# Modulation steps moved ahead of the neighbourhood projections, 14 more PE transposes, and an earlier first normalization in a two-layer diffusion step

## The chip, the cores and the metric

The kernel runs on one core of one Trainium2 chip. The metric is the device time of one execution in microseconds (us), the median of the runs shown. The kernel computes in single precision: every float32 operand of a matmul is split into a high and a low part in fp32r, and each product is made of two or three fp32r matmuls.

## The reference, cut to what matters

Two layers work on 384 tokens (128 context tokens and 256 latent tokens, width 1024). Each layer is a half-step SwiGLU FFN, a mixer with three branches, and a second half-step FFN. Every one of these six sublayers first normalizes and modulates its input with a shift and a scale, and multiplies its result by a gate; these come from a conditioning vector by a matrix of 1024 x 9216 in each layer:

```
m = silu(cvec) @ w_ada[l] + b_ada[l]          # split in 9: shift, scale, gate of three sublayers
h = ln_plain(x) * (1 + scale) + shift
x = layernorm(ALPHA * x + 0.5 * gate * swiglu(h), g, b)           # FFN
u = h @ w_in                                                       # mixer
q   = (rmsnorm(u_q) * g) @ w_uq;      k_nope, v = (rmsnorm(u_kv) * g) @ w_ukv      # latent attention
q_n, k_n, v_n = u_na                                               # neighbourhood attention
x = layernorm(ALPHA * x + gate * ((g_f*y_f + g_m*y_m + g_n*y_n) @ w_out), g, b)
```

The product with `w_ada` is wanted for two vectors only (context and latent).

## The kernel before, in words

The 384 tokens are three tiles of 128. The six sublayers run one after the other on TensorE (PE); the tail of one and the head of the next are interwoven in `transition`. All of PSUM is one ring of 8 banks (`psum`), which every matmul group, transpose or not, takes a bank of, until VectorE (DVE) and ScalarE (ACT) have read it.

**Weights.** Every weight comes as a unit: a load on the SP queue (`_load`, L180), a cast to the high part on ACT (`_high`, L188, `whi`), a subtraction for the low part on DVE (`_low`, L193, `wlo`). A first, dry pass records in which order instructions are issued, and a planner places each load and each split some us of PE time ahead of its first use, as far as 26 buffers of 4 KB per partition ("u4") and 22 of 3 KB ("t3") have room. The SP queue keeps this written order, and a load whose buffer is not free holds up all behind it. The other queues are put in order by the framework's scheduler, which takes work roughly in the order in which it was issued and runs ready work of later issue in gaps; in `begin` PE, ACT and DVE keep the written order too.

**Modulation steps.** Shift, scale and gate of all sublayers but the first are computed on DVE, one eighth of a block of 1024 columns at a time. One `ada_step` loads 128 rows of `w_ada` (512 KB on SP, planned 14 us of PE time ahead) and updates two accumulators `acc`, one for each conditioning vector: a multiply (TENSOR_SCALAR) in the first step of a shift or scale block, else a multiply-add (SCALAR_TENSOR_TENSOR). After the eighth step `ada_finish` transposes and sums both accumulators on DVE, and some calls later `ada_place` makes one small matmul and four small additions. `ada_spend(n)` first does such outstanding finishes and then up to `n` steps from the budget of the sublayer: 36 in the first FFN, 12 in the mixer of layer 0, 8 in that of layer 1. When a shift or scale block ends ahead of a gate block, `gate_start` clears two accumulators on GpSimd (POOL) and issues two small loads from its queue.

**The mixer's order.** `mixer_body` turns the latents (`turn_q`, `turn_kv`), does the Fourier branch (`four_tokens`, `four_channels`), makes the queries (`query`, 3 tiles), the keys (`kn`, four pairs of heads), the values (`v`, four tiles), then the Fourier branch's projection (`yb`, 8 chunks of 12 matmuls, each copied by DVE into `mg`), then latent attention with the gates' matmuls as filling, the neighbourhood values (`value`, `nv`), and the neighbourhood projections of queries and keys (`nq`, `nk`), then neighbourhood attention. In each pair of key heads DVE subtracts the low parts `k<-kn` out of PSUM and copies the rotary part `k<-krt`. The kernel before calls `ada_spend(1)` once in each `value`, once ahead of the neighbourhood stage, and once ahead of each of the eight `nq` and `nk` projections: 3 + 1 + 8 = 12 steps in layer 0, and in layer 1 3 + 1 + 4 = 8.

**The start.** `run` has PE transpose the identity 24 times ("warm"), loads x and the conditioning vectors, and `begin` normalizes the three tiles: statistics of both halves of a tile (`bn_stats`), an aggregation, the power -0.5 on POOL (`rstd`), and for tiles 0 and 1 the normalization on ACT (`xn`), issued after the next tile's statistics. Then PE turns tile 0 (`xT`), multiplies the first 128 columns of shift and scale (`ada`), turns tile 1 and 2, and the first FFN's matmuls (`hd`) begin as each eighth of the modulated input is ready. `sel` and `quad` are two small constants made from the identity for the matmul `adat`.

Of the kernel before, what the change touches and what calls it, by code (L numbers as in the profile page):

```python
# [8 lines left out]
F32 = mybir.dt.float32  # L9
F32R = mybir.dt.float32r  # L10
AF = mybir.ActivationFunctionType
ALU = mybir.AluOpType
AX = mybir.AxisListType
# [3 lines left out]
P = 128  # L17
# [71 lines left out]
class Kernel:  # L89
# [279 lines left out]
    def ada_setup(self):  # L369
        self.ada_blocks = [("g", (0, 0)), ("m", (0, 1), 0), ("m", (0, 1), 1), ("g", (0, 1)), ("m", (0, 2), 0), ("m", (0, 2), 1),  # L370
                           ("g", (0, 2)), ("m", (1, 0), 0), ("m", (1, 0), 1), ("g", (1, 0)), ("m", (1, 1), 0), ("m", (1, 1), 1),
                           ("g", (1, 1)), ("m", (1, 2), 0), ("m", (1, 2), 1), ("g", (1, 2))]
        self.ada_pos, self.ada_fin, self.ada_due = 0, [], []
        self.mod = {}
        self.gate_d = {}
        sel = self.fixed([P, 32], F32, "sel")
        self.nc.vector.tensor_reduce(out=sel, in_=self.ident.rearrange("p (q r) -> p r q", q=4), op=ALU.add, axis=AX.X)
        self.quad = self.fixed([P, 4, 32], F32, "quad")
        self.nc.gpsimd.tensor_copy(out=self.quad, in_=sel.unsqueeze(1).broadcast_to([P, 4, 32]))
        self.bad = [self.fixed([P, 72], F32, "bad") for _ in range(DEPTH)]  # L380

    def ada_bias(self, l):
# [240 lines left out]
    def transition(self, prev, nxt, mod):  # L623
# [65 lines left out]
            p()  # L689
        self.inhead = False  # L690

    def begin(self, nxt):
        nc = self.nc
        hf = [self.slot([P, 2, TOK], F32, "hf") for _ in range(4)]
        ns, mvs, rs = [], [], []

        def normal(t):
            n = self.slot([P, D], F32, "xn")
            if t == NT - 1:
                nc.vector.tensor_scalar(out=n, in0=self.x[t], scalar1=mvs[t][:, 0:1], scalar2=rs[t], op0=ALU.subtract, op1=ALU.mult)  # L700
            else:
                mr = self.small(1)
                nc.vector.scalar_tensor_tensor(out=mr, in0=mvs[t][:, 0:1], scalar=-1.0, in1=rs[t], op0=ALU.mult, op1=ALU.mult)
                nc.scalar.activation(out=n, in_=self.x[t], func=AF.Identity, scale=rs[t], bias=mr)
            ns.append(n)

        for t in range(NT):
            mvs.append(self.stats(self.x[t]))
            rs.append(self.rstd(mvs[t][:, 1:2], 1.0, 1e-6))
            if t:  # L710
                normal(t - 1)

        def turn(t, then=None, qs=range(2)):
            for q in qs:
                pt = self.psum("xT")
                for b in range(4):
                    dc = q * 4 + b
                    nc.tensor.transpose(pt[:, b * P:(b + 1) * P], ns[t][:, dc * P:(dc + 1) * P], self.ident)
                if then and q == 0:
                    then()  # L720
                for b in range(2):
                    o, i = hf[2 * q + b][:, :, t * P:(t + 1) * P], pt[:, b * 256:b * 256 + 256].rearrange("p (a b) -> p a b", a=2)
                    if b:
                        nc.scalar.copy(out=o, in_=i)
                    else:
                        nc.vector.tensor_copy(out=o, in_=i)

        piece = {0: 1, 1: 1, 2: 1, 3: 1, 4: 2, 6: 2}
        m = self.mod_tile((0, 0))

        hg = {}

        def shift(dc, *cds):
            h = hf[dc // 2][:, dc % 2]
            if dc not in hg:
                hg[dc] = self.slot([P, TOK], F32, "hg")
            g = hg[dc]
            for cd in cds:
                c = (slice(0, P), slice(P, TOK))[cd]
                sc, sh = m[:, 1, dc, cd:cd + 1], m[:, 0, dc, cd:cd + 1]  # L740
                nc.scalar.activation(out=self.hm[0][:, dc, c], in_=h[:, c], func=AF.Identity, scale=sc, bias=sh)
                nc.vector.tensor_scalar(out=g[:, c], in0=h[:, c], scalar1=sc, scalar2=sh, op0=ALU.mult, op1=ALU.add)
            for cd in cds:
                c = (slice(0, P), slice(P, TOK))[cd]
                nc.vector.tensor_tensor(out=self.hm[1][:, dc, c], in0=g[:, c], in1=self.hm[0][:, dc, c].bitcast(F32), op=ALU.subtract)

        turn(0)
        self.ada_bias(0)
        normal(NT - 1)
        self.held = []  # L750
        ahead = self.ada_first(0, 1)
        nxt.cold_unit(0)
        turn(1, self.high)
        self.ada_first_finish(0, 1, ahead)
        shift(0, 0)
        turn(2, qs=[0])
        shift(0, 1)
        self.low()
        turn(2, qs=[1])
        every = [(t, g) for t in range(NT) for g in range(HG)]  # L760
        for dc in range(KD):
            d1 = dc + 1
            if d1 < KD:
                nxt.cold_unit(d1)
            if dc:
                parts, i, j = [(p, t, g) for t, g in every for p in range(3)], 6, 9
            else:
                parts, i, j = [(p, t, g) for ps, ts in (((0, 1), (0,)), ((0, 1), (1, 2)), ((2,), range(NT))) for p in ps for t in ts for g in range(HG)], 12, 15
            if not dc:
                self.high()  # L770
                self.low()
            nxt.cold_head(dc, parts[:i])
            self.high()
            self.low()
            if d1 in piece:
                ahead = self.ada_first(d1, piece[d1])
            nxt.cold_head(dc, parts[i:j])
            if d1 in piece:
                self.ada_first_finish(d1, piece[d1], ahead)
            if d1 < KD:  # L780
                shift(d1, 0, 1)
            nxt.cold_head(dc, parts[j:])
            while self.held:
                self.high()
                self.low()
        self.held = None
        nxt.cold_finish()
        self.ada_bias(1)
        self.gate_start()
# [179 lines left out]
    def mixer_body(self, ph):  # L969
        nc, I, K, O, l = self.nc, self.I, self.K, self.O, ph.l  # L970
# [60 lines left out]
            ckT.append(kt)  # L1031

        def query(t):
            c = slice(t * P, (t + 1) * P)
            qk = self.slot([P, NH, HQ], F32, "qtok")
            for hh in range(2):
                b = self.psum("q")
                for kc in range(3):
                    w = self.W(("wuq", l, kc), "mla_w_uq", l, kc * P, 1, 0, 768)
                    self.mm3(b[:, 0:384], (qnT[kc][:, 0, c], qnT[kc][:, 1, c]),  # L1040
                             tuple(x[:, 0, hh * 384:hh * 384 + 384] for x in w), kc == 0, kc == 2)
                bv = b[:, 0:384].rearrange("p (h j) -> p h j", h=4)
                qs = qk[:, 4 * hh:4 * hh + 4]
                if t == 0:
                    nc.scalar.copy(out=qs, in_=bv)
                else:
                    nc.scalar.copy(out=qs[:, :, 0:64], in_=bv[:, :, 0:64])
                    self.rope(qs[:, :, 64:96], bv[:, :, 64:96], t - 1, 4)
            qtok.append(qk)
# [11 lines left out]
        k96 = [self.slot([HQ, 2, 512], F32R, "k96") for _ in range(NH)]  # L1061
        w = self.ukv(l, 0)
        for pr in range(4):
            b = self.psum("kn")
            for kc in range(2):
                lhs = tuple(x[:, kc, 2 * pr:2 * pr + 2].rearrange("p a b -> p (a b)") for x in w)
                self.mm3(b, lhs, (ckT[kc][:, 0], ckT[kc][:, 1]), kc == 0, kc == 1)
            for e in range(2):
                kk = k96[2 * pr + e]
                self.split(kk[0:64, 0], kk[0:64, 1], b[64 * e:64 * e + 64, :])  # L1070
                nc.vector.tensor_copy(out=kk[64:96], in_=krt[64:96].bitcast(F32))
        w = self.ukv(l, 1)
        vm = []
        for t in range(4):
            b = self.psum("v")
            for kc in range(2):
                self.mm3(b, (ckT[kc][:, 0, t * P:(t + 1) * P], ckT[kc][:, 1, t * P:(t + 1) * P]),
                         tuple(x[:, kc].rearrange("p a b -> p (a b)") for x in w), kc == 0, kc == 1)
            vm.append(self.split_v(b))
# [74 lines left out]
        for p2 in range(4):  # L1154
            for nme in ("nq", "nk"):
# [6 lines left out]
                if nme == "nq":  # L1162
                    q = self.slot([P, 2, TOK], F32R, "qN")
# [101 lines left out]
    def run(self):  # L1265
        nc, I, K, O = self.nc, self.I, self.K, self.O
# [6 lines left out]
        self.mhalf = self.fixed([P, 1], F32, "mhalf")  # L1273
        nc.vector.memset(self.mhalf, -0.5)

        wp = self.psum("warm")
        for i in range(24):
            nc.tensor.transpose(wp[:, i % 4 * P:i % 4 * P + P], self.ident, self.ident)
        self.mask = self.fixed([P, 64], F32, "mask")
        self.rp = self.fixed([P, 2, 2, 32], F32, "rp")  # L1280
        self.ada_setup()
# [292 lines left out]
```

## Time and profile before

| | us |
|---|---|
| median of 3 runs (1868.36 to 1870.40) | 1869.28 |
| the profiled execution, whole | 1866.74 |
| its span from first to last instruction | 1865.0 |
| PE busy in the span | 1842.9 |
| DVE busy | 1409.0 |
| ACT busy | 785.3 |
| POOL busy | 94.7 |

The mean granted TensorE clock is 0.997 of full. A timeline row gives start and duration in us, engine, line, operation, what is written and read, the count of merged instructions, and in brackets the idle time of the engine ahead of it with what ended it. Most operations are recorded under L77, the helper that issues them, so they are told apart by their tiles.

### The profile page before, as it was taken

To read this page: it belongs to the slowest core of one execution; us is meant where nothing else is said; L and a number is where in the kernel's file an instruction comes from. 1 tells how busy PE (TensorE), PEld (TensorE's weight loads), DVE (VectorE), ACT (ScalarE), POOL (GpSimd) and SP (SyncE) were. 2 spreads that over 40 slices of the span, in tenths; PEclk is the share of its full clock that TensorE was granted. 3 is DMA by queue.
4 is the path that set the end of the run, shared out by engine and by line. 5 is a ranking of instruction groups with operands and counts; after the bars stand their busy time and mean duration, and the time that the engine had idled before them with its cause. 6 is when DMAs were issued, how large, how long until landed. Compare 5 with 4: busy or idle time off the path is not lost. (4 is left out here: it accounts for less than half of the span.)

```text
span 1865.0 us, 27258 instructions
## 1 busy us (share of the span) xinstructions
PE 1842.9 (99%) x10568; PEld 1728.1 (93%) x10568; DVE 1409.0 (76%) x2206; ACT 785.3 (42%) x1305; POOL 94.7 (5%) x115
## 2 busy tenths in 40 slices
PE   8999999999999999999999999999999999999998
PEld 6899998999899999999999999989999998999997
DVE  6788888689997677888876888978798776533345
ACT  4433335556355453332453333355554553533330
POOL 0000002000100010000000000120001000000000
PEclk9999999999999999999999999999999999999999
DMA  9766656234835446666545666542356353444522
GB/s 325 264 224 212 206 209 207 88 102 126 234 109 188 125 148 221 196 226 219 188 159 186 221 220 219 193 157 89 113 177 183 104 190 130 133 135 125 145 92 79
DMA packets 225602, 320.22 MB, mean 172 GB/s; under 512 B 32784, under 2 KB 181888, under 8 KB 225344
## 3 DMA queue, kind: packets, MB, share of 16 engines
q1 hardware_dynamic: 223328, 313.88, 52.5%
q0 software_dynamic: 2112, 4.59, 0.6%
q8 instruction: 83, 1.36, 0.3%
q14 instruction: 47, 0.39, 0.1%
q10 hardware_dynamic: 32, 0.01, 0.0%
HBM read 312.32 MB, written 8.02 MB: 172 GB/s over the span
## 5 line engine op out<-in xcount | busy, mean ns | idle before, releaser
L193 DVE TENSOR_TENSOR wlo<-raw,whi 128x1024 fp32r<-128x1024 f32 (+4 forms) x420 | 488.7, 1181 | 148.7 <-ACT whi L188 68.0
L188 ACT CAST whi<-raw 128x1024 fp32r<-128x1024 f32 (+4 forms) x420 | 420.3, 1020 | 325.9 <-DVE wlo L193 83.7
L77 PE MATMUL w<-hmh,whi 128*128 128x384 f32 x1152 | 388.3, 337 | 0.8 <-ACT sl L77 0.8
L77 PE MATMUL w<-hmh,wlo 128*128 128x384 f32 x1152 | 387.1, 336 | 0.0
L77 PE MATMUL w<-hml,whi 128*128 128x384 f32 x1152 | 387.1, 336 | 0.0
L77 PE MATMUL y<-whi,sT 128*128 128x512 f32 x1050 | 335.1, 391 | 1.7 <-DVE sT L77 1.5
L77 DVE SCALAR_TENSOR_TENSOR acc<-raw,cs,acc 128x1024 f32<-128x1024 f32 x236 | 296.9, 1290 | 28.8 <-DMA raw<-in_w_ada_dram 28.5
L77 PEld LDWEIGHTS y<-whi,sT 128*128 128x128 f32 x1050 | 196.8, 188 | 41.1 <-DVE sT L77 2.1
L77 PEld LDWEIGHTS w<-hmh,whi 128*128 128x128 f32 x1152 | 216.6, 188 | 3.2 <-ACT sl L77 1.1
L77 PEld LDWEIGHTS w<-hml,whi 128*128 128x128 f32 x1152 | 216.6, 188 | 1.9
L77 PEld LDWEIGHTS w<-hmh,wlo 128*128 128x128 f32 x1152 | 216.6, 188 | 0.0
L77 PE MATMUL y<-wlo,sT 128*128 128x512 f32 x525 | 204.2, 389 | 0.0
L77 PE MATMUL g<-hmh,whi 128*128 128x384 f32 x384 | 132.5, 345 | 1.4 <-DVE qN L77 1.4
L77 PE MATMUL g<-hmh,wlo 128*128 128x384 f32 x384 | 129.8, 338 | 1.6 <-DVE wlo L193 1.6
L77 PE MATMUL g<-hml,whi 128*128 128x384 f32 x384 | 129.9, 338 | 0.0
L77 PEld LDWEIGHTS y<-wlo,sT 128*128 128x128 f32 x525 | 98.6, 188 | 18.1
L77 ACT CAST sT<-sl 128x384 fp32r<-128x384 f32 x72 | 37.1, 515 | 183.8 <-DVE sl L77 183.8
L77 PE MATMUL hd<-whi,hmh 128*128 128x256 f32 (+1 forms) x336 | 100.1, 300 | 1.6 <-ACT hmh L77 1.6
L77 PE MATMUL hd<-wlo,hmh 128*128 128x256 f32 (+1 forms) x336 | 99.0, 297 | 0.0
L77 PE MATMUL hd<-whi,hml 128*128 128x256 f32 (+1 forms) x336 | 98.9, 296 | 0.0
L77 ACT ACTIVATE sl<-w 128x384 f32<-128x384 f32 x72 | 35.4, 492 | 110.0 <-PE w L77 109.7
L77 POOL TENSOR_TENSOR st<-st,mhalf 128x1 f32<-128x1 f32 x48 | 43.9, 916 | 689.3 <-DVE st L77 689.2
(271 smaller groups left out, 2952.3 us busy)
## 6 DMA issues: line engine op xcount, KB each, us to landing
raw<-in_ffn_w_dram SPq DMA_DIRECT2D x244, 512.0 KB, 5.0
raw<-in_w_ada_dram SPq DMA_DIRECT2D x128, 512.0 KB, 4.9
raw<-in_w_gate_dram SPq DMA_DIRECT2D x48, 512.0 KB, 4.1
raw<-in_w_in_dram SPq DMA_DIRECT2D x32, 512.0 KB, 6.1
raw<-in_w_ada_dram SPq DMA_DIRECT2D x32, 256.0 KB, 5.9
raw<-in_w_out_dram SPq DMA_DIRECT2D x16, 512.0 KB, 6.8
raw<-gd SPq DMA_DIRECT2D x12, 512.0 KB, 5.1
raw<-in_ffn_w_dram SPq DMA_DIRECT2D x22, 256.0 KB, 5.8
```

The lines of the kernel that those rows point to most:

```text
L77: r = f(*a, **kw)
L188: self.real.scalar.copy(out=hi, in_=r)
L193: self.real.vector.tensor_tensor(out=lo, in0=r, in1=hi.bitcast(F32), op=ALU.subtract)
```

## The change

Three edits. The nine calls of `ada_spend` that come new in `mixer_body` use up the budgets of 12 and 8 earlier: in layer 0 three steps stand ahead of the queries, four ahead of the key pairs, two ahead of values 1 and 3, and the last three in `value` as before; in layer 1 three, four and one, and none is left for `value`. The calls further down stay, with nothing to spend. In `begin` PE transposes the identity 14 more times before anything else of `begin`, tile t-1 is normalized between the two halves of tile t's statistics rather than after them, and `sel` and `quad` are computed after the statistics.

```diff
 ada_setup:
-        sel = self.fixed([P, 32], F32, "sel")
-        self.nc.vector.tensor_reduce(out=sel, in_=self.ident.rearrange("p (q r) -> p r q", q=4), op=ALU.add, axis=AX.X)
+        self.sel = self.fixed([P, 32], F32, "sel")
         self.quad = self.fixed([P, 4, 32], F32, "quad")
-        self.nc.gpsimd.tensor_copy(out=self.quad, in_=sel.unsqueeze(1).broadcast_to([P, 4, 32]))
+    def warm(self, n):
+        wp = self.psum("warm")
+        for i in range(n):
+            self.nc.tensor.transpose(wp[:, i % 4 * P:i % 4 * P + P], self.ident, self.ident)
+
     def begin(self, nxt):
         nc = self.nc
+        self.warm(14)
...
         for t in range(NT):
-            mvs.append(self.stats(self.x[t]))
+            st = self.small(12)
+            for h in range(2):
+                nc.vector.bn_stats(out=st[:, h * 6:h * 6 + 6], in_=self.x[t][:, h * 512:h * 512 + 512])
+                if t and h == 0:
+                    normal(t - 1)
+            mvs.append(self.moments(st, 2))
             rs.append(self.rstd(mvs[t][:, 1:2], 1.0, 1e-6))
-            if t:
-                normal(t - 1)
+        nc.vector.tensor_reduce(out=self.sel, in_=self.ident.rearrange("p (q r) -> p r q", q=4), op=ALU.add, axis=AX.X)
+        nc.gpsimd.tensor_copy(out=self.quad, in_=self.sel.unsqueeze(1).broadcast_to([P, 4, 32]))
...
         def query(t):
+            self.ada_spend(1)
...
         for pr in range(4):
+            self.ada_spend(1)
             b = self.psum("kn")
...
         for t in range(4):
+            self.ada_spend(t % 2)
             b = self.psum("v")
...
 run:
-        wp = self.psum("warm")
-        for i in range(24):
-            nc.tensor.transpose(wp[:, i % 4 * P:i % 4 * P + P], self.ident, self.ident)
+        self.warm(24)
```

## Rows read from the trace of the kernel before

**Rows 1.** The page: busy us of each engine in the span.
```profile
PE 1842.9 (99%) x10568; PEld 1728.1 (93%) x10568; DVE 1409.0 (76%) x2206; ACT 785.3 (42%) x1305; POOL 94.7 (5%) x115
```

**Rows 2.** Stretches: PE, PEld, DVE, ACT, POOL busy (count), granted clock, DMA share, GB/s.
```profile
0.00:20.00 20.00, 14.73 (x88) 11.68 (x92) 12.73 (x38) 8.43 (x15) 2.60 (x10) 0.91 1.00 297
500.00:520.00 20.00, 16.96 (x96) 16.27 (x95) 20.00 (x38) 7.54 (x16) 8.37 (x6) 0.91 0.53 144
1380.00:1500.00 120.00, 120.00 (x754) 116.74 (x753) 98.14 (x209) 61.25 (x128) 8.44 (x7) 1.00 0.49 151
```

**Rows 3.** Timeline: waits at layer 0's neighbourhood attention; the stretch behind them.
```profile
508.58 0.42 PE L77 MATMUL g<-hmh,whi 128*128 128x384 f32 x1 [1.40 <-DVE qN L77]
510.82 0.45 PE L77 MATMUL g<-hmh,wlo 128*128 128x384 f32 x1 [1.64 <-DVE wlo L193]
510.00:516.00 6.00, 5.18 (x21) 5.18 (x22) 6.00 (x8) 0.27 (x1) 2.48 (x1) 0.72 0.36 122
```

**Rows 4.** The chain of waits in layer 1's keys: start, us, engine and tile.
```profile
1287.82 0.69 DVE k L77
...
1299.28 0.68 DVE k L77
...
1300.10 14.80 PE yb L77 x84
```

**Rows 5.** Stretches with DVE alone: DVE busy (count), clock, DMA share, GB/s.
```profile
341.00:379.22 38.22, 32.10 (x77) 1.00 0.28 90
1261.00:1299.26 38.26, 32.12 (x78) 1.00 0.28 92
395.00:460.00 65.00, 55.39 (x117) 1.00 0.42 119
320.00:341.00 21.00, 10.86 (x31) 1.00 0.29 82
```

**Rows 6.** Timeline, DVE: a finish, a first step, a pair of multiply-adds.
```profile
477.31 1.23 DVE L77 STREAM_TRANSPOSE at<-acc 128x1024 f32<-128x1024 f32 x1
...
479.63 1.21 DVE L77 TENSOR_REDUCE red<-at 128x32 f32<-128x1024 f32 x1
...
481.92 0.71 DVE L77 TENSOR_SCALAR acc<-raw,cs 128x1024 f32<-128x1024 f32 x1
...
484.33 2.48 DVE L77 SCALAR_TENSOR_TENSOR acc<-raw,cs,acc 128x1024 f32<-128x1024 f32 x2
```

**Rows 7.** Timeline, SP and DVE: layer 0's mixer; the page's landing of modulation loads.
```profile
335.77 0.34 SPq L180 DMA_DIRECT2D raw<-in_mla_w_uq_dram  x1
...
345.12 51.67 SPq L180 DMA_DIRECT2D raw<-in_w_gate_dram  x8
...
381.69 1.88 DVE L77 TENSOR_TENSOR vs<-v,vs 128x512 fp32r<-128x512 f32 x3
...
raw<-in_w_ada_dram SPq DMA_DIRECT2D x128, 512.0 KB, 4.9
```

**Rows 8.** The first 14 us: transposes by tile, timeline rows, loads with their landing.
```profile
L77 PE MATMUL warm<-ident x24: 272/421/477, 1.4 to 6.2; 128*128 128x128 f32 x24
...
6.26 0.55 POOL L77 TENSOR_TENSOR st<-st,mhalf 128x1 f32<-128x1 f32 x1 [4.95 <-DVE st L77]
...
8.17 1.24 ACT L77 ACTIVATE xn<-x,st,st 128x1024 f32<-128x1024 f32 x1 [1.26 <-DVE st L77]
...
9.47 1.97 PE L77 MATMUL xT<-ident,xn 128*128 128x128 f32 x8 [2.84 <-ACT xn L77]
...
11.49 1.73 PE L77 MATMUL ada<-raw,cs 128*32 128x256 f32 x16
13.14 1.09 PE L77 MATMUL xT<-ident,xn 128*128 128x128 f32 x8
...
2.62 2.19 SPq L180 DMA_DIRECT2D raw<-in_w_ada_dram  x4
...
raw<-in_w_ada_dram SPq DMA_DIRECT2D x14, 256.0 KB, 6.1
```

## The prediction, on record before the run

> **What bounds the kernel now.** I read the page's busy times first: PE works 99% of the span [rows 1], so only 22.1 us (1865.0 - 1842.9) of PE idle time, and stretches at the lower of the clock's two levels, are there to be won; everything else can only be lost. I then cut the span into stretches to find where they lie. Two stand out [rows 2]: the first 20 us, with 5.27 us idle and a mean clock of 0.91, and 500 to 520, with 3.04 us idle and 0.91. The reader is to see that nothing of the kind shows in layer 1's copy of the second place: from 1380 to 1500 PE has no idle time at full clock. The third view is the chain of waits through the stage in which the moved steps come to stand, and it is the one that decides. From 1287.82 to 1299.96 the chain does not run over PE but over DVE, from one subtraction `k<-kn` to the last, and from there straight to PE's `yb` at 1300.10 [rows 4]: the bank ring is full, chunk 1 of the Fourier projection waits until the last key pair has been read out. DVE is the bound there for 12 us, in the middle of a kernel that is bound by PE. In layer 0 the stage has the same shape: DVE is busy for 32.10 us up to its last key subtraction, in layer 1 for 32.12 [rows 5].
>
> **The change part by part.**
>
> *Steps taken out of the neighbourhood stage.* Layer 0's nine steps with their finish leave DVE between 460 and 516. There PE waited 1.40 us for `qN` and 1.64 us for a weight split, and from 510 to 516 the mean granted clock is 0.72 [rows 3]: a share of 2 x 0.28 = 0.57 of the 6 us, 3.4 us, at 1.2 instead of 2.4 GHz. PE was busy nearly all of that time, so it lost half, 1.7 us. With the 3.04 us idle [rows 2] that is 4.7 us. With over 20 us of DVE work (nine steps) gone from there nothing else is near being late, so I take all of it; from below 3.0, if the clock falls all the same. In layer 1 there is nothing to gain [rows 2], and POOL's clearing of gate accumulators, which moves along, has an engine at 5% [rows 1]. The eight emptied calls cost nothing, they issue no instruction.
>
> *Steps put ahead of queries, keys and values.* Before DVE can make the last `k<-kn`, seven steps now stand ahead of it in the order of issue. Layer 0: steps 5 to 8 of one block, 8 multiply-adds at 2.48 / 2 = 1.24 us, 9.9; then the finish of that block, two transposes of 1.23 and two sums of 1.21, 4.9; a first step of two multiplies of 0.71, 1.4; two more steps, 5.0. Sum 21.2 us [rows 6]. Layer 1: seven steps of multiply-adds, 14 x 1.24 = 17.4 us.
> What hides them is idle time on DVE between the landing of the first of their loads and that last subtraction. The loads are planned 14 us of PE time ahead, just behind the third `wuq` load, and this one leaves SP only at 335.77, when its buffer comes free [rows 7]. With 4.9 us to landing [rows 7] the first step can run at 341. From there to 379.22 DVE is busy for 32.10 of 38.22 us, 6.1 idle; in layer 1 32.12 of 38.26, 6.1 [rows 5]. I let the scheduler fill every one of these gaps. What is left comes ahead of the chain [rows 4] one for one: 21.2 - 6.1 = 15.1 us in layer 0, 17.4 - 6.1 = 11.3 in layer 1.
> Behind it come two more steps in layer 0 (5.0 us) and one with a finish in layer 1 (2.5 + 4.9 = 7.4), ahead of the splits of values 1 to 3. These have room: the last value split ended at 383.6 [rows 7], and the bank that it frees is wanted four chunks after the one that waits, chunks of 14.80 / 7 = 2.1 us [rows 4], so at about 388.4. Of 4.8 us of room 0.2 and 2.6 us are overdrawn. PE also idles for over ten us, where 1.4 + 1.6 sufficed for the lower clock [rows 3], and the first 3.4 us behind the wait cost 1.7; DVE catches up meanwhile, so the larger of the two counts: 1.7 and 2.6. Layer 0 loses 16.8, layer 1 13.9, together 30.7 us. Bounds: no more than the overdraft (0) if the scheduler lets the key splits pass; 42 us if no gap is filled (12.2 us more).
> The nine loads of 512 KB in layer 0 have DMA to spare, its share is 0.28 from 341 to 379 [rows 5]. They go into SP's queue ahead of branch and gate weights; the gate loads wait there for buffers until 396.8 in any case [rows 7]. I set nothing for it and keep the risk for a rival. The three steps left in layer 0's `value` stay where DVE has 9.6 idle us in 65 [rows 5]; layer 1's go from there, where PE has no wait to lose.
>
> *The 14 transposes and the earlier normalization.* The 24 transposes have a median of 421 ns, the last of them 272: the clock came up while they ran. PE then idles 2.84 us, and the turning of tile 0 takes 1.97 us where the next takes 1.09: the clock was down again [rows 8]. At the full level's 1.09 / 8 = 0.14 us at most 14 transposes take 1.9 us, ending near 8.4. The power of tile 0 is ready on POOL at 6.81, but its normalization starts on ACT at 8.17, behind tile 1's second statistics and `sel` [rows 8]; put between the halves it can start at about 7.1, and tile 0 is turned from 8.4 instead of 9.47, to 9.5 instead of 11.44. The next matmuls want the four `w_ada` loads issued by 4.81; the last, issued near 4.4 with 6.1 us to landing, arrives near 10.5 [rows 8]. From there the 1.73 us of `ada` become about 1.1 at full clock: done at 11.7 instead of 13.2, 1.5 us earlier. Behind it PE follows a chain of short steps on DVE and ACT that moves along. `sel` and `quad` (0.7 us) go to an idle place. I take 1.5; from below 0, if a later landing takes it back, from above 2.3 (5.27 idle us are there [rows 2]).
> The Trainium skill, TensorE: Matmul & The Clock Gate (Part 4: PE-mode transpose), says that transposes do not count as work for the clock, so that the full level does not engage for them; that speaks against the 14. Here 24 transposes, with nothing else on PE, ended at 272 ns after a median of 421 [rows 8], so the trace disagrees. By the page the gain would be the earlier start alone, 10.5 + 1.7 against 13.2, 1.0 us.
>
> Sum: -4.7 - 1.5 + 30.7 = +24.5 us. The profiled execution took 1866.74 us (1865.0 in the span and 1.7 around it), so 1891.2; the median of the runs is 2.5 us above it, so 1893.8, rounded to 1894.
>
> **The rivals.**
> *A. The steps find room; only the gains are left (chance 0.22).* If the scheduler puts key splits ahead of waiting steps, or loads land late enough, the steps slide into the 9.6 idle us of latent attention and into pauses in which DVE waits for ACT. For it: 10.1 us of DVE stand idle just before 341 [rows 5], which an earlier load would reach, and DVE's order is not strictly that of issue. Against it: SP releases nothing before 335.77 [rows 7], and DVE was already the chain [rows 4]. Time: 1869.3 - 6.2 = 1863, from 1861 to 1865.5.
> *B. Half of it (0.08).* Three or four of the seven steps come behind the last key split: about 6 us lost in the two layers together, as much as is won. Within 0.2% of 1869.3, which is 3.7 us and about what a measurement of this kernel can tell from no change.
> *C. The loads do harm too (0.12).* Nine more u4 buffers are taken where SP already waits 51.67 us over eight gate loads [rows 7]; branch weights then come late and PE waits for a weight split on top of the keys. It decides from the point where SP reaches the branch loads later than some 15 us after 337. At another 5 us in each layer: 1904.
> *D. The 14 transposes do not hold the clock.* It changes the sum by 0.5 us and is in the range.
>
> **How the numbers follow.** The forecast, DVE's extra work lands on the key splits, has 0.58: 1894, its own range 1878 (three of seven steps behind the last key split in each layer, 7.4 us twice) to 1906 (the gaps not filled). With C, slower has 0.70; B gives 0.08 for the same; A 0.22 for faster. The range that holds 8 in 10 has to take in A: 1862 to 1905.
>
> **What would show it.** Right: a PE wait of 10 to 16 us at the first chunks of `yb` in both layers, ended by DVE `k`, with `acc` rows back to back on DVE ahead of it; a lower granted clock behind the wait; no wait at 505 to 516; xT from about 8.4 and no lower clock before 13. Wrong: `acc` rows behind the key splits or spread ahead of 341, PE without idle time through `kn`, `v` and `yb`; then the time is A's. If the keys are on time but PE waits for weights, it is C.

## The result, and the profile after

The changed kernel takes 1892.63 us (median of 4 runs, 1891.51 to 1893.47), the kernel before 1868.82 beside it: a ratio of 1.0128, 95% interval 1.0110 to 1.0145. It is slower, as forecast (1894), by a little less than forecast. The profiled execution took 1893.47 us, with 1891.7 in the span, 26.7 more than before.

The page's busy row, the answer to [rows 1]: PE works 7.3 us longer for the same matmuls and 14 transposes, and idles 41.5 us instead of 22.1; DVE has no more to do than before.

```profile
PE 1850.2 (98%) x10582; PEld 1733.7 (92%) x10582; DVE 1405.1 (74%) x2206; ACT 784.4 (41%) x1305; POOL 94.3 (5%) x115
```

Where the time came from is read off the start of the same matmul in both traces. Each interval's own cost is the difference between neighbouring lines of the last column:

| first matmul of | before | after | shift | what the interval cost |
|---|---|---|---|---|
| `uf`, layer 0 (Fourier branch) | 314.92 | 313.49 | -1.43 | the start: -1.43 |
| `s`, layer 0 (latent attention) | 394.72 | 411.41 | +16.69 | layer 0's keys: +18.12 |
| neighbourhood `s`, layer 0 | 505.57 | 522.23 | +16.66 | -0.03 |
| `nkO`, layer 0 (behind the gates' matmuls) | 524.71 | 536.44 | +11.73 | neighbourhood stage: -4.93 |
| `wo`, layer 0 | 632.82 | 643.53 | +10.71 | -1.02 |
| `uf`, layer 1 | 1234.86 | 1245.70 | +10.84 | +0.13 |
| `s`, layer 1 | 1314.73 | 1341.64 | +26.91 | layer 1's keys: +16.07 |
| `wo`, layer 1 | 1546.90 | 1573.63 | +26.73 | -0.18 |

The stretches that answer to [rows 2] and [rows 5], all in the columns of [rows 2]. In the first 20 us no stretch at the lower level is recorded, in the neighbourhood stage PE idles no more, layer 1's neighbourhood is as it was. The fourth and fifth run up to the last subtraction of a key: DVE has 1.2 us idle in 52 and 0.9 in 50, PE 13.6 and 8.6. The last two are the lower level, 1.2 GHz, behind the waits of each layer.

```profile
0.00:20.00 20.00, 16.84 (x113) 13.06 (x113) 13.17 (x39) 8.77 (x15) 2.60 (x10) 1.00 1.00 297
517.00:537.00 20.00, 20.00 (x127) 19.64 (x126) 12.46 (x37) 8.06 (x20) 0.00 (x0) 1.00 0.52 143
1406.91:1526.91 120.00, 120.00 (x753) 116.73 (x752) 81.30 (x194) 61.46 (x128) 9.04 (x7) 1.00 0.42 119
341.00:393.10 52.10, 38.49 (x202) 33.47 (x200) 50.86 (x94) 21.64 (x42) 1.46 (x1) 0.90 0.38 137
1271.84:1321.67 49.83, 41.20 (x222) 36.59 (x220) 48.95 (x92) 22.14 (x43) 1.46 (x1) 0.93 0.43 143
389.60:396.40 6.80, 3.15 (x10) 3.18 (x11) 6.61 (x12) 3.57 (x6) 0.00 (x0) 0.51 0.24 80
1331.60:1335.00 3.40, 3.23 (x10) 3.27 (x11) 3.40 (x7) 0.00 (x0) 0.00 (x0) 0.50 0.50 154
```

PE's waits over the whole span (us in total, times, longest). All four lie in the keys. The first stood at 0.8 us in the kernel before, the other three are new; so are 1.3 us at `fa` and 0.6 at `fo`, in the Fourier branch ahead of the keys, also for results of DVE:

```profile
PE yb L77 <- DVE k L77: 11.4, 3, 5.8
PE ada L77 <- DVE red L77: 6.2, 1, 6.2
PE yb L77 <- DVE vs L77: 3.2, 2, 2.8
PE qT L77 <- DVE k L77: 3.0, 2, 2.0
```

Layer 0's keys on PE, from the timeline: three waits, and the third ends 0.15 us after the last key is read out.

```profile
377.37 0.66 PE L77 MATMUL ada<-red,quad 128*128 128x64 f32 x2 [6.16 <-DVE red L77]
...
388.11 0.50 PE L77 MATMUL qT<-ident,qtok 128*96 128x128 f32 x3 [1.99 <-DVE k L77]
393.25 0.98 PE L77 MATMUL yb<-oF,whi 128*128 128x384 f32 x2 [4.64 <-DVE k L77]
```

DVE in the same place. Between the second and the third key subtraction stand a finish (transposes, sums) and a first step, back to back; behind each later pair stands a step, up to the last subtraction, which ends at 393.10 instead of 379.91:

```profile
372.03 0.69 DVE L77 TENSOR_TENSOR k<-kn,k 64x512 fp32r<-64x512 f32 x1
372.64 2.36 DVE L77 STREAM_TRANSPOSE at<-acc 128x1024 f32<-128x1024 f32 x2
374.93 2.30 DVE L77 TENSOR_REDUCE red<-at 128x32 f32<-128x1024 f32 x2
377.15 1.40 DVE L77 TENSOR_SCALAR acc<-raw,cs 128x1024 f32<-128x1024 f32 x2
378.58 0.68 DVE L77 TENSOR_TENSOR k<-kn,k 64x512 fp32r<-64x512 f32 x1
...
387.89 2.46 DVE L77 SCALAR_TENSOR_TENSOR acc<-raw,cs,acc 128x1024 f32<-128x1024 f32 x2
...
392.41 0.69 DVE L77 TENSOR_TENSOR k<-kn,k 64x512 fp32r<-64x512 f32 x1
```

Layer 1, PE and then DVE: a second wait behind the keys, for a value split that stands behind a finish.

```profile
1316.67 0.98 PE L77 MATMUL yb<-oF,whi 128*128 128x384 f32 x2 [5.78 <-DVE k L77]
...
1331.77 0.98 PE L77 MATMUL yb<-oF,whi 128*128 128x384 f32 x2 [2.78 <-DVE vs L77]
```

```profile
1320.98 0.69 DVE L77 TENSOR_TENSOR k<-kn,k 64x512 fp32r<-64x512 f32 x1
...
1326.43 2.36 DVE L77 STREAM_TRANSPOSE at<-acc 128x1024 f32<-128x1024 f32 x2
1328.72 2.30 DVE L77 TENSOR_REDUCE red<-at 128x32 f32<-128x1024 f32 x2
1330.94 1.28 DVE L77 TENSOR_TENSOR vs<-v,vs 128x512 fp32r<-128x512 f32 x2
```

The start, the answer to [rows 8]: the turning of tile 0 follows the 14 transposes at full clock, and `ada` waits for its last load.

```profile
6.89 1.88 PE L77 MATMUL warm<-ident 128*128 128x128 f32 x14
8.61 1.04 PE L77 MATMUL xT<-ident,xn 128*128 128x128 f32 x8
...
11.09 0.64 PE L77 MATMUL ada<-raw,cs 128*32 128x256 f32 x8 [0.81 <-DMA raw<-in_w_ada_dram]
```

### The profile page after: what moved, and what is told of

Its sections match the earlier page's. It is cut to its first block, busy times and chain, and to the rows that moved or that the text cites. A ratio compares the mean times of both kernels' runs of the same rounds, so it can differ in the third digit from the quotient of the medians.

```text
span 1891.7 us, 27275 instructions
## 1 busy us (share of the span) xinstructions
PE 1850.2 (98%) x10582; PEld 1733.7 (92%) x10582; DVE 1405.1 (74%) x2206; ACT 784.4 (41%) x1305; POOL 94.3 (5%) x115
```

## The experiments

The theory is the prediction's: every us of step work that is issued ahead of the last key's subtraction delays PE by one us, once DVE's idle time is used up. Rivals: the loads do it (prediction's C), the finish and the ring of banks do it, or moving steps costs the same anywhere.

**The two halves, each alone.** `begin_only` is the changed kernel without the three new calls:

```diff
         def query(t):
-            self.ada_spend(1)
...
         for pr in range(4):
-            self.ada_spend(1)
...
         for t in range(4):
-            self.ada_spend(t % 2)
```

> The changed kernel without the nine new calls of ada_spend: only the 14 transposes, the earlier normalization and the moved constants stay. Theory K (DVE's added work stands ahead of the key splits and PE waits for it): all of the loss goes, what is left is the gain at the start, 1.4 us by the two traces: 1867.4, ratio to before 0.9992. Rival S (part of the loss comes from the start, by a different order of everything behind it): well above 1870.

Measured: 1866.34 us, ratio 0.9993 (0.9984 to 1.0001). In its trace it is 1.48 us ahead up to the neighbourhood stage; `nkO` then starts 0.05 later than before. The gain was made and lost again inside that stage (below).

`steps_only` has the three new calls, and the start of the kernel before:

```diff
     def begin(self, nxt):
-        self.warm(14)
...
-            st = self.small(12)
-            for h in range(2):
-                nc.vector.bn_stats(out=st[:, h * 6:h * 6 + 6], in_=self.x[t][:, h * 512:h * 512 + 512])
-                if t and h == 0:
-                    normal(t - 1)
-            mvs.append(self.moments(st, 2))
+            mvs.append(self.stats(self.x[t]))
             rs.append(self.rstd(mvs[t][:, 1:2], 1.0, 1e-6))
+            if t:
+                normal(t - 1)
```

> The kernel before with nothing but the nine new calls. Theory K: 1892.6 + 1.4 = 1894, with the same waits of PE at yb (11.4 us by DVE k) in both layers, and a lower clock again in the first 13 us. Rival S: near 1870.

Measured: 1892.96 us, ratio 1.0134 (1.0116 to 1.0153). The whole loss is the steps'. Layer 0's keys cost 18.75 us, layer 1's 14.58, the neighbourhood stage gives 4.93 back.

**Is it the length of the multiply-adds, or the loads?** `light_steps` leaves all loads, calls and instructions in place; the multiply-adds of the moved steps touch 32 of 1024 columns, so the other columns miss those terms.

```diff
-                nc.vector.scalar_tensor_tensor(out=a, in0=w, scalar=sc, in1=a, op0=ALU.mult, op1=ALU.add)
+                c = slice(0, 32 if light else D)
+                nc.vector.scalar_tensor_tensor(out=a[:, c], in0=w[:, c], scalar=sc, in1=a[:, c], op0=ALU.mult, op1=ALU.add)
```

> The changed kernel, but in the nine moved steps of layer 0 and the eight of layer 1 the multiply-adds work on 32 of 1024 columns (the rest of the accumulators isn't updated); first multiplies, finishes and all loads stay as they are. Theory K: of 21 us ahead of layer 0's last key split some 8 stay (finish 4.7, multiplies 1.4, twelve short ones), which the 6 idle us nearly cover; in layer 1 under 2 of 17. The wait at yb falls to 0 to 4 us, the neighbourhood stage keeps its gain of 5: 1864 to 1869. Rival L (the loads of the moved steps take buffers and SP's queue from the branch weights): stays at 1885 or above.

Measured: 1870.03 us, ratio 1.0008 (0.9999 to 1.0017). Rival C falls: nine 512 KB loads in layer 0 stand where they stood, and layer 1's keys cost 1.32 us instead of 16.07. Shorter steps also give their buffers back earlier, so the second half of the answer is the changed kernel's own trace: PE waits there nowhere for a part of a weight. Layer 0's still cost 9.06, which I had not expected: `s` starts 7.45 later with a start 1.61 ahead. DVE's rows there say why. The finish and the first step are not shortened, and they come between two subtractions, where no idle time is left:

```profile
368.71 0.69 DVE L77 TENSOR_TENSOR k<-kn,k 64x512 fp32r<-64x512 f32 x1
369.32 2.36 DVE L77 STREAM_TRANSPOSE at<-acc 128x1024 f32<-128x1024 f32 x2
371.61 2.30 DVE L77 TENSOR_REDUCE red<-at 128x32 f32<-128x1024 f32 x2
373.83 1.40 DVE L77 TENSOR_SCALAR acc<-raw,cs 128x1024 f32<-128x1024 f32 x2
...
384.59 0.69 DVE L77 TENSOR_TENSOR k<-kn,k 64x512 fp32r<-64x512 f32 x1
```

The last subtraction ends at 385.28; before, in this kernel's frame, at 379.91 - 1.61 = 378.30: 6.98 us later, of which the finish and the step are 5.94 (369.32 to 375.26). The other 2.1 of the 9.06 are about one chunk of `yb`: chunk 0 waits for the last key there, as in the changed kernel.

**Is that chunk a bank of the ring?** `ada_place` takes a bank for one small matmul, between the keys and `yb`. Then chunk 0, not chunk 1, would be the one that waits for the last key. `place_late` puts the placing off, in every stage:

```diff
-        self.ada_due.append([3, lambda: self.ada_place(blk, red)])
+        self.ada_due.append([12, lambda: self.ada_place(blk, red)])
```

> The changed kernel, but the small matmul that places a finished block comes 12 calls after its finish instead of 3, so in layer 0 it no longer stands between the key and the value matmuls and takes no bank there. Theory K with the bank ring: the bank of that matmul moves the waiting chunk of yb from the second to the first, so one chunk (12 matmuls, 2.1 us) is added to the wait; without it layer 0 gets 2 us back, layer 1 nothing: 1890.5. Rival W (PE's wait of 6.2 us at this matmul for DVE's sums is a cost of its own): 1886.5. Rival O (it is hidden under DVE's chain, the bank too): 1892.5.

Measured: 1897.98 us, ratio 1.0159 (1.0145 to 1.0172), so none of the three numbers; but the edit reached further than the question, since it costs 3.6 us ahead of layer 1's keys and makes those cost 19.56. In layer 0 alone the question can be read, and the timeline answers it: chunk 0 waits for an earlier key and chunk 1 for the last one. The keys cost 15.59 us instead of 18.12, though the last subtraction comes no earlier. These 2.5 us are not the chunk alone: behind the wait for the last key the clock is full (1.00 from 394 to 397), where the changed kernel has the lower level up to 396.3.

```profile
389.11 0.98 PE L77 MATMUL yb<-oF,whi 128*128 128x384 f32 x2 [5.44 <-DVE k L77]
...
394.25 0.58 PE L77 MATMUL yb<-oF,whi 128*128 128x384 f32 x2 [1.03 <-DVE k L77]
```

**Less DVE work, same steps.** `krt_on_act` keeps the change and copies the rotary part on ACT; four pairs of heads with two copies of about 0.65 us are taken off DVE in each layer:

```diff
-                nc.vector.tensor_copy(out=kk[64:96], in_=krt[64:96].bitcast(F32))
+                nc.scalar.copy(out=kk[64:96], in_=krt[64:96].bitcast(F32))
```

> The changed kernel with the eight copies k<-krt of each layer on ACT instead of DVE. Theory K: DVE's chain to the last key split loses 8 x 0.65 = 5.2 us in each layer, and PE's wait with it: 1892.6 - 10.4 = 1882, less of it (1886) if ACT's own splits then come late. Rival L: the loads are as late as before, 1892 plus or minus 2. A third, that PE's wait at the small matmul ada for DVE red (6.2 us in layer 0) is a cost of its own: layer 0 gains less than 3 us, layer 1 the whole 5.

Measured: 1882.32 us, ratio 1.0078 (1.0063 to 1.0094). Layer 0's keys cost 10.99 and layer 1's 9.60: 7.1 and 6.5 us came off where 8 x 0.65 = 5.2 went from DVE. So DVE is the bound there, and PE's wait for the finish at `ada` is no cost of its own, which would have left layer 0 a gain under 3. What came off beyond 5.2 was not taken apart; in layer 0 the clock is full from the start of `yb` on, at 387.47, where the changed kernel lost 1.6 us.

**The steps that the idle time does take.** `query_only` drops the calls at keys and values, so three steps stand ahead of the keys in each layer:

```diff
         for pr in range(4):
-            self.ada_spend(1)
...
         for t in range(4):
-            self.ada_spend(t % 2)
```

> The changed kernel with new calls ahead of the queries alone: three steps (7.4 us on DVE) in each layer come ahead of the key splits, the others stay where the kernel before has them. Theory K: DVE's 6 idle us ahead of the last key split take in all but 1 to 2 us in each layer, so the wait at yb is 1 to 2 us in place of 15 and 11, the neighbourhood stage of layer 0 has six steps where it had nine and loses its wait: 1869 - 1.5 - 4.7 + 3 = 1866 (1863 to 1869). Rival P (every step costs its 2.5 us wherever it stands ahead of the keys): 1869 - 6 + 15 = 1878.

Measured: 1865.61 us, ratio 0.9985 (0.9975 to 0.9995). The keys cost 1.43 us in layer 0 and 1.47 in layer 1 for 7.4 us of multiply-adds each. The wait is not where it was expected: at `yb` it is 0.41 us, as before, and PE waits 0.66 us at `fa` and 0.45 at `fo` instead, ahead of the keys. DVE has 1.0 us idle left up to the last subtraction of layer 0, where it had 6.1. The neighbourhood stage gains 4.93, and 2.8 of it go to a later start of that stage, with waits of 1.5 and 0.8 us for the parts of a weight in it. By `uf` of layer 1 it is 3.22 ahead.

**Other places for them.** `begin_40_8` keeps the start and moves four steps of layer 0 to the first FFN's budget:

```diff
-        budget = {(0, 0): 36, (0, 1): 12, (0, 2): 36, (1, 0): 36, (1, 1): 8, (1, 2): 0}
+        budget = {(0, 0): 40, (0, 1): 8, (0, 2): 36, (1, 0): 36, (1, 1): 8, (1, 2): 0}
```

> The start of the changed kernel with no new calls, and four of the mixer's twelve steps of layer 0 moved into the first FFN instead (budgets 40 and 8 for 36 and 12). DVE has 5 to 10 idle us in the last 20 us stretches of that FFN and no bank of PSUM waits for it. Theory K: the neighbourhood stage of layer 0 then has the shape of layer 1's, which has no wait: 1868.7 - 1.5 - 5 = 1862.5 (1861 to 1864). If the four steps and the finish cost PE time at the end of the FFN: 1866 or more.

Measured: 1874.92 us, ratio 1.0035 (1.0022 to 1.0049), a miss. The first FFN asks for no more than 36 steps; the four were made up in one go ahead of the next transition, and PE waited for the finish behind them. The neighbourhood stage gained its 4.93 us all the same. PE's row at the finish, and the stretch behind it, with the clock down:

```profile
638.52 0.66 PE L77 MATMUL ada<-red,quad 128*128 128x64 f32 x2 [13.09 <-DVE red L77]
```

```profile
638.00:652.00 14.00, 13.48 (x52) 11.13 (x53) 4.93 (x12) 4.58 (x6) 0.00 (x0) 0.83 0.57 177
```

`fill_three` keeps the start and puts three calls into latent attention, where DVE had 9.6 idle us [rows 5]:

```diff
+                if d in (1, 3, 5):
+                    self.ada_spend(1)
```

> The new begin, and three modulation calls in the latent attention's fillers (where PE works on) in place of the ones in the transition. By the theory that only the keys' splits pay for moved steps: the wait at the neighbourhood's projections of layer 0 goes (-5 us by the start of wo), the keys cost nothing, 1862 us (1861 to 1864). By the rival that any place in the stretch between pays as much as it gains: 1866 as with the new begin alone.

Measured: 1865.02 us, ratio 0.9981 (0.9972 to 0.9990): faster than the kernel before, but above the 1861 to 1864 that were expected. The keys cost nothing, and from the neighbourhood's `s` to `nkO` it is 4.93 us shorter, without the waits for `qN` and `wlo`. But that `s` starts 5.29 us later: two other waits came ahead of it, at the first `nk`, together 3.3 us, and the clock fell behind them (0.83 over 10 us, so 3.4 us at the lower level, 1.7 us lost).

```profile
476.44 0.44 PE L77 MATMUL nk<-hmh,whi 128*128 128x384 f32 x1 [1.51 <-ACT whi L188]
479.22 0.44 PE L77 MATMUL nk<-hmh,wlo 128*128 128x384 f32 x1 [1.81 <-DVE wlo L193]
```

```profile
480.00:490.00 10.00, 10.00 (x51) 10.00 (x50) 9.97 (x14) 3.90 (x6) 0.00 (x0) 0.83 0.22 66
```

`fill_three_krt` adds the copies on ACT, with the diff of `krt_on_act`:

> The same, with the copies of the rotated key on ACT instead of DVE, which takes two pieces of about 0.43 us off DVE between the keys' splits of each layer. If DVE still ends last at the keys, 0.5 to 1 us a layer come off: 1861 us (1860 to 1863); if not, the time of the run without.

Measured: 1869.23 us, ratio 1.0004 (0.9995 to 1.0013): the other way. The expectation has two copies of 0.43 us in each layer; the edit moves eight, of 0.65 us on DVE and some 1.0 on ACT. With DVE free, ACT became the late engine at the keys. It is busy for 9.76 of the 10 us from 371, five of DVE's eight subtractions in layer 0 now wait 1.0 to 1.8 us for ACT's part of a key, and `yb` waits 1.71 us where 0.41 stood in `fill_three`. The copies paid only while DVE was the chain.

```profile
371.00:381.00 10.00, 7.41 (x39) 6.17 (x38) 5.26 (x7) 9.76 (x13) 0.00 (x0) 1.00 0.16 52
```

```profile
377.29 0.59 PE L77 MATMUL yb<-oF,whi 128*128 128x384 f32 x2 [1.71 <-DVE k L77]
```

**Where did the start's gain go in `begin_only`?** This can be read from one trace of each kernel alone, since the interval of the medians takes in 1. The stage has the same instructions as in the kernel before. One multiply-add is longer: DVE's row and POOL's row from the timeline of `begin_only`, and then the run of four from the kernel before, in which one took 2.42 us:

```profile
506.89 2.88 DVE L77 SCALAR_TENSOR_TENSOR acc<-raw,cs,acc 128x1024 f32<-128x1024 f32 x1
...
506.86 1.82 POOL L77 TENSOR_TENSOR raw<-raw,mask 128x768 f32<-128x768 f32 x1
```

```profile
501.97 6.00 DVE L77 SCALAR_TENSOR_TENSOR acc<-raw,cs,acc 128x1024 f32<-128x1024 f32 x4
...
501.43 1.87 POOL L77 TENSOR_TENSOR raw<-raw,mask 128x768 f32<-128x768 f32 x1 [39.32 <-DMA raw<-rpb]
```

`mask_on_dve` is `begin_only` with POOL's addition of the mask given to DVE:

```diff
-            nc.gpsimd.tensor_tensor(out=tv, in0=tv, in1=self.mask.unsqueeze(1).broadcast_to([P, 12, 64]), op=ALU.add)
+            nc.vector.tensor_tensor(out=tv, in0=tv, in1=self.mask.unsqueeze(1).broadcast_to([P, 12, 64]), op=ALU.add)
```

> The run with the new begin alone, with the additions of the neighbourhood's mask moved from POOL to DVE. If it is POOL's addition beside it that stretched one of DVE's multiply-adds there to 2.88 us, the longest multiply-add of the accumulation into acc is back at about 1.29 us, and the projections of the neighbourhood start 1 to 1.6 us earlier than in that run; if not, one stays at 2.4 us or more. The four additions cost DVE about 1 us each, elsewhere in the same stage.

Measured, in one run: 1862.2 us, under all 21 runs of the kernel before (1865.66 to 1871.28) and all 11 of `begin_only` (1864.16 to 1868.69). The run of four takes 4.86 us instead of 6.00 and no multiply-add over 1.29. `nkO` starts 4.09 us earlier than in `begin_only`, more than expected: with the wait for `qN` down from 1.4 to 0.3 us and the one for `wlo` from 3.3 to 1.6 the clock no longer fell.

```profile
500.62 4.86 DVE L77 SCALAR_TENSOR_TENSOR acc<-raw,cs,acc 128x1024 f32<-128x1024 f32 x4
```

```profile
505.00:510.00 5.00, 3.10 (x25) 2.66 (x22) 5.00 (x8) 0.27 (x1) 1.98 (x4) 1.00 0.38 118
510.00:515.00 5.00, 5.00 (x30) 5.00 (x30) 5.00 (x15) 1.52 (x2) 0.00 (x0) 1.00 0.33 105
```

**The turns and the normalization, each alone.** The turns are the 14 transposes. `normal_only` is `begin_only` without them; `turns_only` has them and the order of the kernel before:

```diff
 normal_only:
-        self.warm(14)
 turns_only:
-            st = self.small(12)
-            for h in range(2):
...
+            mvs.append(self.stats(self.x[t]))
...
+            if t:
+                normal(t - 1)
```

> The changed kernel's begin (first tile normalized between the second's statistics) without the 14 turns, and no step moved into the transition. By the theory that the earlier normalization gives the time and the turns only hold the clock: xT starts some 1.2 us earlier than before, the clock falls once more for a stretch of the first 15 us as in the kernel before, and uf of layer 0 starts 0.5 to 1.1 us earlier (1.43 with the turns). By the rival that the turns do nothing here: uf starts 1.4 us earlier and the clock doesn't fall.

> The kernel before with the 14 additional transposes alone. Read from the trace, by the start of the first uf matmul of layer 0 and the granted clock of the first 15 us. If transposes hold the clock: no stretch at 1.2 GHz from 9 to 13 us, the first eight xT take 1.1 us instead of 1.97, all behind them 0.5 to 1 us earlier. If they don't (a rule of the Trainium skill, TensorE: Matmul & The Clock Gate, Part 4: PE-mode transpose): clock and times as before, 0 us.

Measured, one run each: 1868.38 and 1868.36 us, which tell nothing of terms this small, but the first 315 us do. `uf` starts 1.02 us earlier in `normal_only`, 1.44 later in `turns_only`, 1.48 earlier with both (`begin_only`). The stretches 9 to 11 and 11 to 13, first of `normal_only`, then of `turns_only`: without the turns the clock is at the lower level while tile 0 is turned; with the turns alone it holds through that and falls right behind it (and again at 25 to 30 us, to a mean of 0.68); there PE had waited 2.12 us for the normalization.

```profile
9.00:11.00 2.00, 2.00 (x14) 0.99 (x12) 1.93 (x7) 1.59 (x3) 0.79 (x2) 0.50 1.16 320
11.00:13.00 2.00, 2.00 (x20) 1.14 (x17) 1.68 (x7) 0.92 (x2) 0.00 (x0) 0.69 1.05 379
```

```profile
9.00:11.00 2.00, 1.45 (x17) 1.12 (x17) 1.59 (x6) 1.55 (x2) 0.55 (x1) 1.00 1.15 327
11.00:13.00 2.00, 2.00 (x20) 1.09 (x13) 1.68 (x7) 1.30 (x4) 0.00 (x0) 0.52 1.05 375
```

## Why the prediction was right, and where its terms were off

**The neighbourhood stage: 4.7 forecast, 4.93 measured.** Waits and lower clock went together, and nothing else came late. What the prediction did not see is a part of why DVE was late there: 1.14 us of its run of four and 0.78 of a pair of splits (3.13 us in the kernel before, 2.35 in `mask_on_dve`) were time lost beside POOL's additions. In the one run of `mask_on_dve` the stage is 2.70 us shorter than in the kernel before with no step moved, and PE's waits are down to 0.3 us for `qN` and 1.6 for `wlo`.

**The start: 1.5 forecast, 1.43 measured.** Tile 0 is turned from 8.61 (forecast 8.4), the last load ends the wait at 11.09 (10.5), `ada` ends at 11.73 (11.7). That the last two agree is in part luck: the load is 0.6 us later than forecast, but half of `ada` runs ahead of it, so 0.64 us follow it and not 1.1. Rival D, that the turns do not hold the clock, is refuted by the stretches from 9 to 11; its price of 0.5 us was right, they are worth 1.48 - 1.02 = 0.46. The 1.0 us that the prediction drew from the Trainium skill, TensorE: Matmul & The Clock Gate (Part 4: PE-mode transpose), is what the run without the turns gives; with 14 transposes more, the stretch from 9 to 11 goes from 0.50 to 1.00, so here the trace disagrees with that page.

**The keys: 15.1 and 11.3 forecast; 14.6 and 10.9 measured** at the last subtraction. It ends at 393.10 where 379.91 - 1.43 was due, and at 1321.67 where 1299.95 + 10.84 was. Counting seven steps ahead of the key chain, less the idle time, was the right account. That it came out to half a us is in part luck, since both of its terms were too large. Up to the last subtraction DVE still idles 1.2 us in layer 0 and 0.9 in layer 1, so 4.9 and 5.2 us of the 6.1 were filled; and with the delay of 14.6 and 10.9 the steps added 19.5 and 16.1 us of busy time, not 21.2 and 17.4. `query_only` agrees in the same way (7.4 us of multiply-adds less 6.1 leave 1.3; 1.43 and 1.47 measured, with 5.2 us filled in layer 0), and `light_steps` shows that it is the work, not its loads.

**Behind the keys: 1.7 and 2.6 forecast; 3.5 and 5.2 measured.** This is the term that was mis-sized. In layer 0 the prediction let chunk 1 of `yb` wait for the last key, as in the kernel before; the placing of the finished block takes one bank more, so chunk 0 waits, and 2.1 us are added to the 1.6 that the lower clock costs (half of 393.25 to 396.40). In layer 1 it let the larger of two counts stand, overdraft or clock; they add up: 0.42 + 2.78 us of waits for values, and half of the 3.4 us at the lower clock, 4.9 of the 5.2. The prediction's upper bound for both layers, 42 us, is 30.7 + 12.2 = 42.9.

**The rest.** Forecast for the span: +24.5; measured: +26.7, with -1.02 us between `nkO` and `wo` of layer 0 that the prediction did not have. It stands in `steps_only` and `light_steps` too, and not in `begin_only`. 0.42 us of it is a wait in the kernel before, where DVE makes a finish ahead of the operand of `oT`; neither the finish nor the wait is there in the changed kernel. The rest stays open.

```profile
593.10 0.81 PE L77 MATMUL yb<-oT,whi 128*128 128x384 f32 x3 [0.42 <-ACT oT L77]
```

That the median came out under the forecast, by 1.4 us, is luck: the profiled execution, 2.5 us under its median before, lies 0.84 above it after.

**The rivals.** A and B fall with the rows above: the steps stand between the key subtractions, not behind them. The sign that the prediction named, a wait of 10 to 16 us at the first chunks of `yb`, ended by `k`, did not come as it was put. At `yb` PE waits 4.6 us for `k` in layer 0 and 6.8 in layer 1. The 12.8 us of layer 0 are spread: 6.2 of them stand at the small matmul `ada`, for the finish, and 2.0 at a transposition `qT`. The prediction had no wait of PE for the finish. C falls with `light_steps`, and with PE's waits in the changed kernel. Still open: what the later placing costs outside layer 0's keys in `place_late`; and what the mask on DVE would give together with three steps elsewhere, which was not run.

## What to carry to other kernels

A step moved to "idle" time costs nothing only as far as the idle time between its data's arrival and the next instruction that someone waits for goes: here 4.9 and 5.2 of 6.1 idle us were filled, about two of seven steps, and the rest came one for one. Count the banks of a shared ring that a moved step takes, since they shift which later group waits. Before work is moved out of a late stage, compare each instruction there with its own median: the stage may be late because of one that is stretched, not because there is too much.

## What the runs showed of the hardware

A DVE multiply-add with two SBUF inputs and POOL's addition of two SBUF inputs hold each other up. The multiply-add that met the addition took 2.88 us (2.42 in the kernel before) where its median is 1.28, and ended 1.1 us after POOL did; where DVE was first, with a multiply-add from 508.36 and a split behind it, POOL's addition took 3.69 us, where the one from 501.43 took 1.87 (kernel before).

```profile
508.78 3.69 POOL L77 TENSOR_TENSOR raw<-raw,mask 128x768 f32<-128x768 f32 x1 [0.45 <-DMA raw<-rpb]
```

With no addition on POOL the longest of 22 was 1.29 (the accumulations of `begin_only`, then of `mask_on_dve`; count, then shortest, median and longest in ns).

```profile
L77 DVE SCALAR_TENSOR_TENSOR acc<-raw,cs,acc x22: 1267/1275/2885, 433.1 to 514.0; 128x1024 f32<-128x1024 f32 x22
```

```profile
L77 DVE SCALAR_TENSOR_TENSOR acc<-raw,cs,acc x22: 1270/1276/1285, 433.3 to 511.3; 128x1024 f32<-128x1024 f32 x22
```

The Trainium skill, SBUF — State Buffer (Who interferes with whom), says that a DVE instruction with two SBUF inputs contends with a GpSimd instruction that reads SBUF, since its second input comes through a read interface that the two share, and that the order of issue decides which one blocks. The runs agree, with 2.88 us on DVE in the one order and 3.69 on POOL in the other. Which pair meets depends on a us or two: PE's wait for `wlo` is 3.3 us in the two traces with a start over 1 us earlier (`begin_only`, `normal_only`) and 1.6 in the kernel before and in `turns_only`, one trace of each.
